# First projection of a two-layer decoder trunk: x in quarters, its weights in smaller transfers, casts between the evacuations

## The chip, the cores and the metric

One core of a Trainium2 chip. The metric is the device time of one execution in microseconds (us). The profile of the kernel before is one execution, recorded by the hardware profiler. Engines are called PE (matmul; PEld is its weight load), DVE (vector), ACT (scalar), POOL (gpsimd) and SP (which here only issues transfers).

## The reference

Two layers, each with RMSNorm, one input projection, three causal token mixers, an output projection, then RMSNorm and a gated MLP with a short convolution. All in float32, 256 tokens, width 1024. Only the first step of the first layer matters here:

```python
h = rmsnorm(x, norm1_g[i])                    # (1, 256, 1024)
(a_q, a_kc, ...) = jnp.split(h @ w_in[i], IN_OFFSETS, axis=-1)   # w_in[i]: 1024 x 2615
```

## The kernel before, in words

The 256 tokens are two tiles (t) of 128 partitions. `xr` holds x as tokens x 1024. For a projection PE needs x with its columns on the partitions, so `transposed` (L184) transposes 128-column blocks (four PE transposes for two blocks and two token tiles, into one PSUM bank of role "t", "s" or "o"), and evacuates each block: ACT writes `hi` (rounded to fp32r, times the norm's gain; L195), DVE writes the remainder `lo` (L196). Weights are split in the same way by `weight` (L148): a transfer on SP into a staging buffer `st` (five of them, NST), an ACT cast to `hi` (L158), a DVE subtraction for `lo` (L160). A staging buffer can be filled again when both have read it. `mm3` (L205) makes one product out of three: hi x hi, hi x lo, lo x hi.

The input projection runs in seven column blocks, by `project` (L273): block 0 has columns 0 to 384, the second (336 columns, `put_a1`) 384 to 720, the third (360 columns, `put_i`) 1103 to 1463, and so on. Each has four weight transfers (two 128-row pieces each) and 48 matmuls in eight steps k (two token tiles x three products). `fill` advances these generators a step at a time, between other work.

The norm's row scale isn't applied to x but at the evacuation of each block: `sumsq` (ACT, L179) and L258 (DVE) sum the squares of x, `rms` and `scales` make `rstd` and its multiples on POOL (L172 to L174, L265), and the `put_...` functions use them.

At the start, in layer 0: x comes in halves of columns, token tile by token tile; PE runs 16 idle matmuls on zeros (`idle`), transposes the gain columns (`columns`, L141), then the first half of x (L239, L242), then 8 more idle matmuls. Step 0 and 1 of block 0 follow (`fill(1)`, L569), then `second_half` transposes the second half of x behind the newest matmul, and the squares come behind its evacuations. The casts of the second block's weights are put behind the squares: `behind=squares` (L562), where `squares[0]` is the last of ACT and `squares[1]` the last of DVE.

The order on each engine is planned ahead by the framework's scheduler from the program's order and dependences, and is fixed when the kernel runs. `after(ins)` puts what the block issues behind `ins` on the engine of `ins`.

Of the kernel before, what the change touches and what calls it, by code (L numbers as in the profile page):

```python
# [12 lines left out]
F32 = mybir.dt.float32  # L13
FR = mybir.dt.float32r
# [6 lines left out]
D = 1024  # L21
# [5 lines left out]
AHEAD = 5  # L27
NST, NHL = 5, 8
# [42 lines left out]
def trunk(ctx, tc, x, norm1_g, w_in, cmp_pos, cmp_w1, cmp_w2, w_out, norm2_g, w_up, conv_w, conv_b, w_down,  # L71
          final_g, eye, consts_f, consts_b, out):
    nc = tc.nc
# [12 lines left out]
    turn = [0]  # L86
# [9 lines left out]
    xr = keep.tile([128, 2, D], F32, name="xr")  # L96
    ident = keep.tile([128, 128], F32, name="ident")
    rn = keep.tile([16, 128], F32, name="rows_n")
    nc.sync.dma_start(xr[:, 0, 0:512], x[0, 0:128, 0:512])
    nc.scalar.dma_start(xr[:, 1, 0:512], x[0, 128:256, 0:512])  # L100
    nc.sync.dma_start(ident, eye)
    nc.scalar.dma_start(rn, norm1_g.rearrange("l (f p) -> (l f) p", p=128))
    zero = keep.tile([128, 256], BF, name="zero")
    V.memset(zero, 0.0)
# [40 lines left out]
    def after(ins):  # L145
        return tc.issue_after(ins) if ins else nullcontext()
# [13 lines left out]
            V.tensor_sub(lv, sv, hv.bitcast(F32))  # L160
        return hv, lv

    def w_in_chunk(i, c0, n, then=(None,) * 4, behind=(None, None)):
        w = w_in[i].rearrange("(k p) c -> p k c", p=128)
        return [weight(w[:, 2 * h:2 * h + 2, c0:c0 + n], 2, n, then[h], behind) for h in range(4)]


    def rms(ss, name):
# [12 lines left out]
    def new_ssq():  # L181
        return keep.tile([128, 2, 2], F32, name="ssq", tag="ssq", bufs=2)

    def transposed(bank, src, gain, hi, lo, k0, nk, role="t"):  # L184

        b = bank(role)
        for j in range(nk):
            for t in range(2):
                PE.transpose(b[:, j * 256 + t * 128:j * 256 + (t + 1) * 128],
                             src[:, t, (k0 + j) * 128:(k0 + j + 1) * 128], ident)  # L190
        h, l = (z[k0 // 4][:, k0 % 4:k0 % 4 + nk, :] for z in (hi, lo))
        for j in range(nk):
            g = gain[:, k0 + j:k0 + j + 1]
            bj = b[:, j * 256:(j + 1) * 256]
            l0 = S.activation(h[:, j, :], bj, AF.Copy, scale=g)  # L195
            l1 = V.scalar_tensor_tensor(l[:, j, :], bj, g, h[:, j, :].bitcast(F32), op0=OP.mult, op1=OP.subtract)  # L196
        return l0, l1

    def act_half():
# [10 lines left out]
    for i in range(DEPTH):  # L210

        with ExitStack() as es:
# [5 lines left out]
            tmp = es.enter_context(tc.tile_pool(name="tmp", bufs=2, reuse_waits="tile"))  # L218

            w2 = pj.tile([128, 2, 64], F32, name="w2")  # L220
            first, squares = None, [None, None]
            if i == 0:

                def idle(n):
                    b = bank("d")
                    for j in range(n):
                        PE.matmul(b[:, :256], zero[:, 0:128], zero, start=j == 0, stop=j == n - 1)

                idle(16)
                columns(bank("t"), cola[:, 0:16], rn)  # L230


                def other_half():
                    for t in range(2):
                        nc.sync.dma_start(xr[:, t, 512:D], x[0, t * 128:(t + 1) * 128, 512:D])

                ssq = new_ssq()
                hhi, hlo = act_pair()
                two = transposed(bank, xr, gain1[i], hhi, hlo, 0, 2, role="t")  # L239
                first = w_in_chunk(0, 0, 384, (other_half, None, None, lambda: nc.sync.dma_start(cf, consts_f)),  # L240
                                   [z.ins for z in two])
                transposed(bank, xr, gain1[i], hhi, hlo, 2, 2, role="s")  # L242
                idle(8)
            rstd = None
            rs8, rs16, rsh = (pj.tile([128, 2], F32, name=f"rs{j}") for j in range(3))

            def second_half(behind):

                with after(behind):
                    for k0 in (4, 6):  # L250
                        last = transposed(bank, xr, gain1[0], hhi, hlo, k0, 2, role="so"[k0 // 2 - 2])
                for t in range(2):
                    with after(last[0].ins):
                        squares[0] = sumsq(ssq, t, 0).ins
                    junk = pj.tile([128, 512], BF, name="junkv", tag="selb")
                    xs = xr[:, t, 512:D]
                    with after(last[1].ins):
                        squares[1] = V.scalar_tensor_tensor(junk, xs, 1.0, xs, op0=OP.mult, op1=OP.mult,  # L258
                                                            accum_out=ssq[:, t, 1:2]).ins

            def scales():
                nonlocal rstd
# [7 lines left out]
                    if i == 0:  # L270
                        other_constants()

            def project(c0, n, done, wh=None, behind=(None, None), role="d"):  # L273
                wh = wh or w_in_chunk(i, c0, n, behind=behind)
                bs = [bank(role), bank(role)]
                for half in range(4):
                    for t in range(2):
                        for k in range(2):
                            kk = half * 2 + k
# [274 lines left out]
            def put_qk(r, dst):  # L554
                def put(t, b):
# [3 lines left out]
                    return lambda: evac(dst(t), turned([P_[:, a * 128:(a + 1) * 128] for a in range(3)]))  # L559
                return put  # L560

            dense += [project(0, 384, put_a0, first), project(384, 336, put_a1, behind=squares, role="s"),  # L562
                      project(1103, 360, put_i),
                      project(719, 384, put_b),
                      project(1463, 384, put_qk(lambda: rs8, lambda t: qT[:, t])),
                      project(1847, 384, put_qk(lambda: rstd, lambda t: kT[:, :, t, :])),
                      project(2231, 384, lambda t, b: a_put(vd[:, t, :], b[:, :384], rstd, t))]
            if i == 0:
                fill(1)  # L569
                second_half(newest[0].ins)  # L570
                scales()
                fill(17 + AHEAD)
            else:
                scales()
                fill(18 + AHEAD)
            V.tensor_scalar(gate, gate, 0.5, 0.5, op0=OP.mult, op1=OP.add)
            gt = gate.rearrange("p t (h c) -> p t h c", c=3)

# [453 lines left out]
```

## Time and profile before

| | us |
|---|---|
| median of 3 runs (lowest, highest) | 664.06 (661.97, 664.2) |
| the profiled execution | 662.68 |
| its span, first to last instruction | 660.9 |
| PE busy in the span | 641.7 |

Each row of the views below is one instruction or a run of equal ones. `bd<-hl,ahi` is the tile written and the tiles read; `[0.88 <-DVE qrT L521]` is idle time of the engine ahead of the instruction and what ended it. `SPq`, `POOLq` and a DMA_DIRECT2D on POOL are the issue of a transfer, not the transfer.

### The profile page before, as it was taken

What the parts mean: (1) busy time and instruction counts of PE and PEld (TensorE: products, weight loads), DVE (VectorE), ACT (ScalarE), POOL (GpSimd) and SP (SyncE); (2) the same over time, 40 slices, a digit from 0 to 9 for tenths busy, and PEclk for the clock granted to TensorE, in tenths of its full rate; (3) what the DMA queues carried; (4) which work ended last, traced back from release to release, by engine and by line L of the source; (5) the groups of instructions that cost most, each with busy time, mean ns of one, the idle gap of its engine ahead of it and who ended that gap; (6) DMA issues with size and microseconds to landing.
All of it is one profiled execution on the core that took longest, in us unless ns stands there. A gap on an engine that the chain in (4) does not pass through costs nothing.

```text
span 660.9 us, 11729 instructions
## 1 busy us (share of the span) xinstructions
PE 641.7 (97%) x4403; PEld 578.4 (88%) x4403; DVE 497.5 (75%) x1093; ACT 375.5 (57%) x683; POOL 50.3 (8%) x119
## 2 busy tenths in 40 slices
PE   8989999999999999999999999999999999999995
PEld 6978987779999999999898888877999999999994
DVE  5979998776766677777587799986697776666653
ACT  6666667775544444455475676785654455544523
POOL 0522210001000000000020242000000000000002
PEclk9999999999999999999999999999999999999998
DMA  8982423454665565565457525234465655566601
GB/s 268 279 265 72 126 83 113 134 184 158 192 188 185 179 188 184 182 182 160 128 167 228 149 71 176 81 110 155 127 218 189 184 182 182 187 191 190 191 1 63
DMA packets 76535, 107.34 MB, mean 162 GB/s; under 512 B 3717, under 2 KB 63414, under 8 KB 76480
## 3 DMA queue, kind: packets, MB, share of 16 engines
q1 hardware_dynamic: 75568, 104.77, 51.2%
q0 software_dynamic: 448, 1.05, 0.5%
q8 instruction: 34, 0.56, 0.3%
q10 hardware_dynamic: 464, 0.79, 0.3%
q14 instruction: 21, 0.17, 0.1%
HBM read 105.55 MB, written 1.05 MB: 161 GB/s over the span
## 4 chain that ended last, share of the span: by engine, by line
PE 81%; DVE 11%; DMA 2%; issue 2%; ACT 2%; POOL 1%; POOLq 0%; DVEq 0%; ACTq 0%
PE bu L921 13%; PE bu L920 13%; PE bu L919 13%; PE bn L206 6%; PE bn L207 6%; PE bn L208 6%; PE bd L206 5%; PE bd L208 5%; PE bd L207 5%; DVE hl L160 3%; PE bs L352 2%; DMA st<-in_w_in_dram 2%; PE bt L372 2%; PE bt L341 1%; DVE acc L484 1%
## 5 line engine op out<-in xcount | busy, mean ns | idle before, releaser
L160 DVE TENSOR_TENSOR hl<-st,hl 128x1024 fp32r<-128x1024 f32 (+3 forms) x208 | 230.7, 1120 | 97.3 <-ACT hl L158 96.8
L158 ACT CAST hl<-st 128x1024 fp32r<-128x1024 f32 (+3 forms) x208 | 198.0, 970 | 136.4 <-PE bu L921 68.1
L920 PE MATMUL bu<-alo,hl 128*128 128x256 f32 x704 | 199.7, 284 | 1.3 <-DVE alo L196 1.3
L921 PE MATMUL bu<-ahi,hl 128*128 128x256 f32 x704 | 199.0, 283 | 0.0
L919 PE MATMUL bu<-ahi,hl 128*128 128x256 f32 x704 | 197.9, 283 | 0.0
L920 PEld LDWEIGHTS bu<-alo,hl 128*128 128x128 f32 x704 | 135.1, 192 | 2.4 <-DVE alo L196 1.7
L919 PEld LDWEIGHTS bu<-ahi,hl 128*128 128x128 f32 x704 | 134.5, 192 | 1.3 <-ACT ahi L195 0.3
L921 PEld LDWEIGHTS bu<-ahi,hl 128*128 128x128 f32 x704 | 135.1, 192 | 0.0
L206 PE MATMUL bd<-hl,ahi 128*128 128x384 f32 (+2 forms) x256 | 92.9, 367 | 2.3 <-ACT hl L158 1.4
L207 PE MATMUL bd<-hl,ahi 128*128 128x384 f32 (+2 forms) x256 | 91.4, 357 | 0.4 <-DVE hl L160 0.4
L208 PE MATMUL bd<-hl,alo 128*128 128x384 f32 (+2 forms) x256 | 91.2, 356 | 0.0
L206 PE MATMUL bn<-hl,h_hi 128*128 128x512 f32 x176 | 68.9, 392 | 0.0
L207 PE MATMUL bn<-hl,h_hi 128*128 128x512 f32 x176 | 68.6, 391 | 0.0
L208 PE MATMUL bn<-hl,h_lo 128*128 128x512 f32 x176 | 68.4, 390 | 0.0
L206 PEld LDWEIGHTS bd<-hl,ahi 128*128 128x128 f32 x256 | 48.0, 188 | 11.0 <-ACT hl L158 3.0
L207 PEld LDWEIGHTS bd<-hl,ahi 128*128 128x128 f32 x256 | 48.2, 188 | 3.6 <-issue 0.8
L208 PEld LDWEIGHTS bd<-hl,alo 128*128 128x128 f32 x256 | 48.2, 188 | 3.1 <-issue 0.9
L208 PEld LDWEIGHTS bn<-hl,h_lo 128*128 128x128 f32 x176 | 33.0, 188 | 7.4 <-DVE h_lo L943 0.4
L206 PEld LDWEIGHTS bn<-hl,h_hi 128*128 128x128 f32 x176 | 33.1, 188 | 6.6 <-ACT h_hi L942 0.5
L207 PEld LDWEIGHTS bn<-hl,h_hi 128*128 128x128 f32 x176 | 33.1, 188 | 6.0
L931 DVE SCALAR_TENSOR_TENSOR c<-a,colc,c 128x255 f32<-128x255 f32 (+1 forms) x88 | 36.7, 477 | 0.7 <-ACT c L929 0.7
L934 ACT ACTIVATE th<-c 128x512 f32<-128x512 f32 x22 | 13.9, 632 | 35.1 <-DVE c L931 35.1
(242 smaller groups left out, 782.0 us busy)
## 6 DMA issues: line engine op xcount, KB each, us to landing
st<-in_w_up_dram SPq DMA_DIRECT2D x88, 512.0 KB, 3.6
st<-in_w_down_dram SPq DMA_DIRECT2D x44, 512.0 KB, 3.5
st<-in_w_in_dram SPq DMA_DIRECT2D x40, 384.0 KB, 3.8
st<-in_w_out_dram SPq DMA_DIRECT2D x12, 512.0 KB, 3.8
st<-in_w_in_dram SPq DMA_DIRECT2D x8, 360.0 KB, 3.5
st<-in_w_in_dram SPq DMA_DIRECT2D x8, 336.0 KB, 3.6
st<-in_w_out_dram SPq DMA_DIRECT2D x8, 256.0 KB, 3.0
xr<-in_x_dram SPq DMA_DIRECT2D x3, 256.0 KB, 5.9
```

Source lines behind the costliest of these rows:

```text
L158: S.copy(hv, sv)
L160: V.tensor_sub(lv, sv, hv.bitcast(F32))
L206: PE.matmul(b, ahi, whi, start=first, stop=False)
L207: PE.matmul(b, ahi, wlo, start=False, stop=False)
L208: return PE.matmul(b, alo, whi, start=False, stop=last)
L352: PE.matmul(b[:, o:o + nk], qa, ka, start=True, stop=True)
L372: PE.transpose(b[:, j * 128:(j + 1) * 128], P[:, j * 128:(j + 1) * 128], ident)
L919: PE.matmul(o, wa, hhi[k // 4][:, k % 4, :], start=k == 0, stop=False)
L920: PE.matmul(o, wa, hlo[k // 4][:, k % 4, :], start=False, stop=False)
L921: PE.matmul(o, wl, hhi[k // 4][:, k % 4, :], start=False, stop=k == 7)
L931: V.scalar_tensor_tensor(c[:, o + d:o + 256], a[:, o:o + 256 - d], cw[w], c[:, o + d:o + 256], op0=OP.mult, op1=OP.add)
L934: S.activation(th, c, AF.Tanh, scale=0.5)
```

## The change

Block 0 of layer 0 is no longer run by `project`'s loop but written out in `begin`, which is called while the list `dense` is made. x comes in four quarters of 256 columns, both token tiles in one transfer: quarter 0 on SP, quarters 1 to 3 on POOL's queue, with consts_f behind them. `ident` moves from SP to ACT's queue. The weights of quarter 0 come in two transfers of 192 KB, the others in three of 384 KB, all on SP. For each quarter, `transposed` gets a pair of weight pieces (`between`): after each evacuation on ACT the cast of one 384-column piece, after each one on DVE its lo. On PE the transposes of quarter q + 1 are put behind step 2q, ahead of step 2q + 1. The squares come behind the casts of the last quarter. The 8 idle matmuls go. `project` takes the finished banks (`bs`) for block 0 and then only calls `put_a0`; `fill` therefore has four steps less.

```diff
@@ -96,9 +96,13 @@
     xr = keep.tile([128, 2, D], F32, name="xr")
     ident = keep.tile([128, 128], F32, name="ident")
     rn = keep.tile([16, 128], F32, name="rows_n")
-    nc.sync.dma_start(xr[:, 0, 0:512], x[0, 0:128, 0:512])
-    nc.scalar.dma_start(xr[:, 1, 0:512], x[0, 128:256, 0:512])
-    nc.sync.dma_start(ident, eye)
+
+    def x_quarter(q, e):
+        c = slice(q * 256, (q + 1) * 256)
+        e.dma_start(xr[:, :, c], x[0, :, c].rearrange("(t p) c -> p t c", p=128))
+
+    x_quarter(0, nc.sync)
+    nc.scalar.dma_start(ident, eye)
     nc.scalar.dma_start(rn, norm1_g.rearrange("l (f p) -> (l f) p", p=128))
     zero = keep.tile([128, 256], BF, name="zero")
     V.memset(zero, 0.0)
@@ -160,9 +164,9 @@
             V.tensor_sub(lv, sv, hv.bitcast(F32))
         return hv, lv
 
-    def w_in_chunk(i, c0, n, then=(None,) * 4, behind=(None, None)):
+    def w_in_chunk(i, c0, n, behind=(None, None)):
         w = w_in[i].rearrange("(k p) c -> p k c", p=128)
-        return [weight(w[:, 2 * h:2 * h + 2, c0:c0 + n], 2, n, then[h], behind) for h in range(4)]
+        return [weight(w[:, 2 * h:2 * h + 2, c0:c0 + n], 2, n, None, behind) for h in range(4)]
 
 
     def rms(ss, name):
@@ -181,7 +185,8 @@
     def new_ssq():
         return keep.tile([128, 2, 2], F32, name="ssq", tag="ssq", bufs=2)
 
-    def transposed(bank, src, gain, hi, lo, k0, nk, role="t"):
+    def transposed(bank, src, gain, hi, lo, k0, nk, role="t", between=None):
+
 
         b = bank(role)
         for j in range(nk):
@@ -194,6 +199,12 @@
             bj = b[:, j * 256:(j + 1) * 256]
             l0 = S.activation(h[:, j, :], bj, AF.Copy, scale=g)
             l1 = V.scalar_tensor_tensor(l[:, j, :], bj, g, h[:, j, :].bitcast(F32), op0=OP.mult, op1=OP.subtract)
+            if between:
+                sv, hv, lv = (z[:, j] for z in between)
+                with after(l0.ins):
+                    l0 = S.copy(hv, sv)
+                with after(l1.ins):
+                    l1 = V.tensor_sub(lv, sv, hv.bitcast(F32))
         return l0, l1
 
     def act_half():
@@ -218,7 +229,7 @@
             tmp = es.enter_context(tc.tile_pool(name="tmp", bufs=2, reuse_waits="tile"))
 
             w2 = pj.tile([128, 2, 64], F32, name="w2")
-            first, squares = None, [None, None]
+            squares = [None, None]
             if i == 0:
 
                 def idle(n):
@@ -229,26 +240,42 @@
                 idle(16)
                 columns(bank("t"), cola[:, 0:16], rn)
 
-
-                def other_half():
-                    for t in range(2):
-                        nc.sync.dma_start(xr[:, t, 512:D], x[0, t * 128:(t + 1) * 128, 512:D])
-
                 ssq = new_ssq()
                 hhi, hlo = act_pair()
-                two = transposed(bank, xr, gain1[i], hhi, hlo, 0, 2, role="t")
-                first = w_in_chunk(0, 0, 384, (other_half, None, None, lambda: nc.sync.dma_start(cf, consts_f)),
-                                   [z.ins for z in two])
-                transposed(bank, xr, gain1[i], hhi, hlo, 2, 2, role="s")
-                idle(8)
+            first = None
             rstd = None
             rs8, rs16, rsh = (pj.tile([128, 2], F32, name=f"rs{j}") for j in range(3))
 
-            def second_half(behind):
-
-                with after(behind):
-                    for k0 in (4, 6):
-                        last = transposed(bank, xr, gain1[0], hhi, hlo, k0, 2, role="so"[k0 // 2 - 2])
+            def begin():
+
+                w = w_in[0].rearrange("(k p) c -> p k c", p=128)
+                wh = []
+                for h in range(4):
+                    st = wst.tile([128, 1024], F32, name="st", tag="st", bufs=NST)
+                    hl = wst.tile([128, 2048], FR, name="hl", tag="hl", bufs=NHL)
+                    sv, hv, lv = (z.rearrange("p (k n) -> p k n", k=2) for z in (st[:, :768], hl[:, :768], hl[:, 1024:1792]))
+                    for k in range(2) if h == 0 else [slice(0, 2)]:
+                        nc.sync.dma_start(sv[:, k], w[:, k, 0:384] if h == 0 else w[:, 2 * h:2 * h + 2, 0:384])
+                    if h:
+                        x_quarter(h, nc.gpsimd)
+                    wh.append((sv, hv, lv))
+                nc.gpsimd.dma_start(cf, consts_f)
+                bs = [bank("d"), bank("d")]
+                last = [None, None]
+
+                def turn(q):
+                    return transposed(bank, xr, gain1[0], hhi, hlo, 2 * q, 2, role="tsst"[q], between=wh[q])
+
+                turn(0)
+                for kk in range(8):
+                    q, k = kk // 2, kk % 2
+                    for t in range(2):
+                        c = slice(t * 128, (t + 1) * 128)
+                        mm = mm3(bs[t][:, :384], hhi[kk // 4][:, kk % 4, c], hlo[kk // 4][:, kk % 4, c],
+                                 wh[q][1][:, k], wh[q][2][:, k], kk == 0, kk == 7)
+                    if k == 0 and q < 3:
+                        with after(mm.ins):
+                            last = turn(q + 1)
                 for t in range(2):
                     with after(last[0].ins):
                         squares[0] = sumsq(ssq, t, 0).ins
@@ -257,6 +284,7 @@
                     with after(last[1].ins):
                         squares[1] = V.scalar_tensor_tensor(junk, xs, 1.0, xs, op0=OP.mult, op1=OP.mult,
                                                             accum_out=ssq[:, t, 1:2]).ins
+                return bs
 
             def scales():
                 nonlocal rstd
@@ -270,10 +298,13 @@
                     if i == 0:
                         other_constants()
 
-            def project(c0, n, done, wh=None, behind=(None, None), role="d"):
-                wh = wh or w_in_chunk(i, c0, n, behind=behind)
-                bs = [bank(role), bank(role)]
-                for half in range(4):
+            def project(c0, n, done, bs=None, behind=(None, None), role="d"):
+                if bs is None:
+                    wh = w_in_chunk(i, c0, n, behind=behind)
+                    bs, halves = [bank(role), bank(role)], range(4)
+                else:
+                    halves = ()
+                for half in halves:
                     for t in range(2):
                         for k in range(2):
                             kk = half * 2 + k
@@ -559,20 +590,14 @@
                     return lambda: evac(dst(t), turned([P_[:, a * 128:(a + 1) * 128] for a in range(3)]))
                 return put
 
-            dense += [project(0, 384, put_a0, first), project(384, 336, put_a1, behind=squares, role="s"),
+            dense += [project(0, 384, put_a0, bs=begin() if i == 0 else None), project(384, 336, put_a1, behind=squares, role="s"),
                       project(1103, 360, put_i),
                       project(719, 384, put_b),
                       project(1463, 384, put_qk(lambda: rs8, lambda t: qT[:, t])),
                       project(1847, 384, put_qk(lambda: rstd, lambda t: kT[:, :, t, :])),
                       project(2231, 384, lambda t, b: a_put(vd[:, t, :], b[:, :384], rstd, t))]
-            if i == 0:
-                fill(1)
-                second_half(newest[0].ins)
-                scales()
-                fill(17 + AHEAD)
-            else:
-                scales()
-                fill(18 + AHEAD)
+            scales()
+            fill((14 if i == 0 else 18) + AHEAD)
             V.tensor_scalar(gate, gate, 0.5, 0.5, op0=OP.mult, op1=OP.add)
             gt = gate.rearrange("p t (h c) -> p t h c", c=3)
```

## Rows read from the trace of the kernel before

**Rows 1.** The page: the span, and the busy time of each engine with its share and its instructions.

```profile
span 660.9 us, 11729 instructions
PE 641.7 (97%) x4403; PEld 578.4 (88%) x4403; DVE 497.5 (75%) x1093; ACT 375.5 (57%) x683; POOL 50.3 (8%) x119
```

**Rows 2.** Stretches of 20 us: length, busy time of PE, PEld, DVE, ACT and POOL (instructions), granted clock of PE as a share of full speed, busy share of the 16 DMA engines, GB/s.

```profile
0.00:20.00 20.00, 17.02 (x101) 14.98 (x102) 12.37 (x26) 13.09 (x24) 4.31 (x16) 1.00 0.78 253
20.00:40.00 20.00, 16.99 (x120) 15.69 (x122) 16.86 (x49) 12.15 (x25) 6.07 (x12) 1.00 1.01 312
40.00:60.00 20.00, 18.91 (x169) 17.28 (x159) 16.79 (x43) 13.64 (x25) 5.92 (x11) 1.00 0.56 165
```

**Rows 3.** The same columns for single microseconds.

```profile
5.00:6.00 1.00, 1.00 (x10) 0.98 (x11) 0.17 (x1) 0.41 (x1) 0.00 (x0) 1.00 0.64 209
...
7.00:8.00 1.00, 0.00 (x0) 0.00 (x0) 0.50 (x2) 0.70 (x2) 0.00 (x0) 1.00 1.06 398
...
12.00:13.00 1.00, 1.00 (x7) 1.00 (x7) 1.00 (x3) 1.00 (x3) 0.62 (x2) 1.00 0.51 128
...
17.00:18.00 1.00, 1.00 (x8) 1.00 (x7) 1.00 (x3) 1.00 (x3) 0.91 (x2) 1.00 0.12 41
...
19.00:20.00 1.00, 1.00 (x9) 1.00 (x8) 1.00 (x2) 0.34 (x1) 0.83 (x3) 1.00 1.01 354
```

**Rows 4.** The chain of waits from 0 to 50 us: start, us, what. "issue" is time in which nothing that the profile shows was waited for.

```profile
15.11 0.62 DVE junkv L258 x2
...
17.90 0.86 DVE hl L160
...
18.78 5.00 DMA st<-in_w_in_dram
...
37.58 2.13 issue
```

**Rows 5.** The timeline of PE: start, us, line, operation, count.

```profile
1.04 3.56 PE L227 MATMUL bd<-zero 128*128 128x256 bf16 x16 [1.04 <-DVE kbd L635]
...
4.89 0.66 PE L189 MATMUL bt<-ident,xr 128*128 128x128 f32 x4
...
5.82 1.04 PE L227 MATMUL bd<-zero 128*128 128x256 bf16 x8
...
8.27 0.62 PE L206 MATMUL bd<-hl,ahi 128*128 128x384 f32 x2 [1.41 <-ACT hl L158]
...
14.09 0.33 PE L206 MATMUL bd<-hl,ahi 128*128 128x384 f32 x1
...
14.26 0.33 PE L207 MATMUL bd<-hl,ahi 128*128 128x384 f32 x1
...
18.25 0.31 PE L206 MATMUL bs<-hl,ahi 128*128 128x336 f32 x1
...
25.69 0.55 PE L341 MATMUL bt<-ident,PA 128*128 128x128 f32 x3 [0.88 <-DVE qrT L521]
...
39.71 1.95 PE L607 MATMUL bo<-w,raw 128*32 128x128 f32 x64 [2.13 <-issue]
```

**Rows 6.** The timeline of ACT and DVE, 5 to 20 us, the same columns.

```profile
5.00 0.17 DVE L142 COPY cola<-bt 128x16 f32<-128x16 f32 x1 [3.95 <-PE bt L141]
...
5.59 0.47 ACT L195 ACTIVATE ahi<-bt,cola 128x256 fp32r<-128x256 f32 x1 [2.43 <-PE bt L189]
...
7.38 0.83 ACT L158 CAST hl<-st 128x768 fp32r<-128x768 f32 x1 [0.30 <-DMA st<-in_w_in_dram]
...
9.83 0.83 ACT L158 CAST hl<-st 128x768 fp32r<-128x768 f32 x1 [1.24 <-DMA st<-in_w_in_dram]
...
12.58 0.48 DVE L196 SCALAR_TENSOR_TENSOR alo<-bs,cola,ahi 128x256 fp32r<-128x256 f32 x1
...
12.98 0.48 DVE L196 SCALAR_TENSOR_TENSOR alo<-bo,cola,ahi 128x256 fp32r<-128x256 f32 x1
...
13.49 0.48 ACT L195 ACTIVATE ahi<-bo,cola 128x256 fp32r<-128x256 f32 x1
...
13.86 0.62 ACT L179 ACTIVATE junk<-xr 128x512 bf16<-128x512 f32 x1
...
15.24 3.48 ACT L158 CAST hl<-st 128x672 fp32r<-128x672 f32 x5
...
16.36 3.99 DVE L160 TENSOR_TENSOR hl<-st,hl 128x672 fp32r<-128x672 f32 x5
```

**Rows 7.** The timeline of SP's and POOL's queues: issue of transfers (start, us that the issue took; a wait lies in it where the buffer or an earlier transfer isn't ready), and POOL's last memset of the start.

```profile
0.89 0.20 POOL L457 MEMSET acc<- 128x128 f32 x1
...
4.17 1.36 SPq L154 DMA_DIRECT2D st<-in_w_in_dram  x2
...
21.46 0.77 POOL L269 DMA_DIRECT2D w<-in_cmp_w_dram  x1
```

**Rows 8.** Transfers by line: tile and source, queue, count, KB each, median us from issue to landing.

```profile
fg<-in_final_g_dram POOLq DMA_DIRECT2D x1, 512.0 KB, 4.0
...
cb<-in_consts_b_dram POOLq DMA_DIRECT2D x1, 256.0 KB, 8.0
```

## Prediction

> **What bounds the kernel now.** Read the page's busy times first: TensorE (PE) is busy 641.7 of 660.9 us [rows 1]. So there are 19 us of idle PE to win in the whole kernel, and the change touches only the first 18 us of it. Next read the stretches of 20 us [rows 2]: in 0 to 20 PE is busy 17.0 us, but between 20 and 40 it is again only 17.0, with the transfers at 1.01 of the DMA engines' time. From 40 us on PE is nearly full. So two different things limit the start: until 18 us PE waits for its first operands, and from 19 to 38 us the kernel is bound by transfers. The single microseconds [rows 3] show where DMA time is lost ahead of that: the share is 0.64 at 5 us, 0.51 at 12 us and 0.12 at 17 us, and 1.01 from 19 us on. The chain of waits [rows 4] says why 17 us is empty. The squares of x on DVE at 15.11 us are followed by the rest (lo) of the second block's weights, 17.90 to 18.77, which frees a staging buffer, and only then, at 18.78, is the next weight transfer issued. It lands 5.00 us later, and the path stays with weights and DVE up to the PE wait of 2.13 us at 37.58. In the timeline of PE the first projection starts at 8.27 and hands over to the second block at 18.25 without a pause [rows 5].
>
> So the number to forecast is not when PE starts, but when the second block's casts free the staging buffers: in the kernel before, 18.78 us.
>
> **The change part by part.**
>
> **Loads.** The first operands become smaller: one x quarter of 256 KB and 192 KB of weights, in place of 512 KB and 384 KB. Quarters 1 to 3 and consts_f go past SP to POOL's queue. SP had to hold two weight transfers until x had landed (issue at 4.17) [rows 7], which is the dip at 5 us [rows 3]; with four SP transfers fewer ahead of them they go out sooner, and about 0.6 us of lost DMA time is regained. No sum needs it, because the last weights already landed ahead of their use. The total bytes are the same.
>
> How late x quarter 1 lands (X1) is not shown before. The nearest rows are POOL's own transfers: 0.77 us of issue for a 256-row one [rows 7], and landing after 4.0 us (512 KB, quiet) to 8.0 us (256 KB, DMA full) [rows 8]. POOL is free at 1.1 us [rows 7], so X1 lies between 5.1 and 9.1; I take 6.5, nearer to the quiet end, because the DMA engines are filled by fewer bytes at that time. The Trainium skill ("DMA: Bandwidth & Descriptors", section "Anatomy of one DMA — SWDGE (gpsimd) path") fits a POOL transfer as 2.0 us plus bytes over 436 GB/s; by that estimate 2.6 us after a 0.8 us issue, X1 would be 4.5 and never late. The rows, at twice that and more, leave a late X1 possible.
>
> The weights of quarter 1 (H1) have at least 1.12 MB ahead of or in them (x quarter, ident, half blocks, themselves) and, if POOL takes an equal share, 1.9 MB. The kernel before landed its first 384 KB of weights (0.99 MB in) at 7.38 and its second (1.9 MB in) at 9.83 [rows 6], so H1 is 7.4 to 9.8; I take 8.5. The same skill page (section "Issuing engines are not separate DMA queues") says that transfers of all queues run on the same 16 engines and that several queues save issue time only; by it three queues bring nothing here but the 0.6 us.
>
> **Start.** The gain columns still come at 5.00 + 0.17 us, from a transfer that keeps its place on ACT's queue, so the first evacuation starts between 5.19 and 5.59 [rows 6]; I take 5.59. The cast of 384 columns isn't shown: on ACT it lies between the step of a 256-column evacuation, 13.86 - 13.49 = 0.37, and that of a 672-column cast, 3.48 / 5 = 0.70; by width 0.48. On DVE between 12.98 - 12.58 = 0.40 and 3.99 / 5 = 0.80; by width 0.50 [rows 6]. So hi of the first block is ready at 5.59 + 0.37 + 0.48 = 6.5 and lo at 7.0, against 8.27 and 9.26 before. PE starts 1.8 us earlier. The 8 idle matmuls taken away (5.82 to 6.86 [rows 5]) lay in a wait and cost nothing.
>
> **First block.** A step k is 6 matmuls at 14.26 - 14.09 = 0.17 us, 1.04; it ends step 0 at 7.9. After that PE runs: four transposes (0.44 of PE time, 0.60 to the last end), step 1, step 2, transposes, step 3, step 4. But step 2 needs evacuation, cast and lo of the transposes just made: 0.65 + 0.37 + 0.48 + 0.07 + 0.55 = 2.1 us after their start, where PE has work for 0.44 + 1.04 + 0.17 = 1.65. So each turn takes 2.1 + 0.87 = 3.0 us, or 2.8 where PE takes the second hi product ahead (it did so at 8.27 [rows 5]), against 2.5 of work. Step 4 ends at 7.9 + 2 x 2.8 = 13.5. I call this time T4; it is 12.5 with the earliest start and no stall. With X1 at 9.1 it is 9.1 + 5.8 = 14.9; with H1 at 9.8 it is 14.6.
>
> **What is queued behind.** The last quarter's transposes are put behind step 4, the squares behind the last quarter's casts, and the second block's casts behind the squares. Before, the second half of x was transposed after step 0, at 10.2 us, so this chain began early. Now it begins at T4. On ACT: transposes and semaphore 0.65; two evacuations and two casts 2 x (0.37 + 0.48) = 1.7; squares 15.24 - 13.86 = 1.4; first cast of the second block 0.7. On DVE then three lo's at 0.8, the third of which frees the buffer of the last weights of the third block: 2.4. Together 6.9 us: issue at T4 + 6.9 = 20.4 against 18.78 [rows 4]. Behind these casts stand PE (second block) and SP (all later weights); the row scales on POOL follow the squares too, and so slip by the same amount. Break-even is T4 = 11.9; even the earliest case, 12.5, misses it. PE itself ends the first block at T4 + 3.5 = 17.0 instead of 18.25, and then waits for the second block's lo until T4 + 4.5 + 0.8 = 18.8: what is won in the block is idle again.
>
> **Sum.** 20.4 - 18.8 = +1.6 us at the entry of the stretch that is bound by transfers. That passes through: DMA is at 1.01 there, PE waits 2.13 us at 39.71 for work behind weights [rows 4, 5], and later PE has at most 1.1 us of idle in 20 to take it up [rows 2]. The eight casts in place of four (+0.8 us on ACT, +0.5 on DVE) are inside this. The profiled execution took 662.68 us (span 660.9 and 1.8 around it), the median shown is 664.06. So the sum is 664.3 by the profile and 665.7 by the median; I give 665.0.
>
> **The rivals.**
> 1. *The earlier PE start counts, the later weights are hidden.* For it: the wait at 25.69 is only 0.88 us [rows 5], and the DMA engines had holes at 12 and 17 us [rows 3] which the new order may fill differently. PE could then keep 18.25 - 17.0 = 1.2 us: 662.68 - 1.2 = 661.5 by the profile, 662.8 by the median. Against it: the squares must come before the second block's casts in either kernel. Chance 0.18.
> 2. *Slower: x quarter 1 comes late from POOL's queue.* Place: the transposes of the first turn, ahead of step 1 in PE's order, so every later matmul waits. Price: each us of X1 beyond 7.9 is one us of T4. The end of the POOL rows, 9.1, gives +3.0 us; at 10.5, where the queue is starved by SP's 1.5 MB, +4.4: 667.1 by the profile, 668.5 by the median. It decides from X1 = 9.5 on (+3.3). Chance 0.13.
> 3. *The clock.* Without the 8 idle matmuls PE pauses about 1 us before step 0. The first 16 ran 3.56 / 16 = 0.22 us each (1.2 GHz for 256 columns), the later 8 at 0.13 (near 2.4) [rows 5]. If it fell back, 30 matmuls up to T4 would cost 0.15 more each: +4.4, 668. Against it: after the pauses at 8.27 and 39.71 (1.4 and 2.1 us) nothing ran slower, and the granted clock is 1.00 in all these rows [rows 2, 3]. Chance 0.03.
> 4. *A different static order later on.* The order on each engine is planned as a whole, so the waits at 25.69 and 39.71 may vanish or grow: -3 to +3 us about the forecast. Chance 0.12, half each way.
>
> **How the numbers follow.** Forecast 0.54, rivals 0.18, 0.13, 0.03, 0.12. 0.5% (3.3 us) is about what a measurement of this kernel can tell from no change. The forecast's own bounds, T4 of 12.5 to 14.9, are +0.6 to +3.0: all within. Within 0.5%: 0.54 + 0.18 + 0.04 of the fourth = 0.76. Slower: rivals 2 and 3 and a part of 4, 0.18. Faster than that needs the first rival and both later waits gone (1.2 + 0.9 + 2.1): 0.06. The range runs from rival 1 by the profile, 661.5, to rival 2 by the median, 668.5.
>
> **What would show it.** Right: first projection matmul near 6.5; the last transposes of x near 13.5; squares on ACT near 15.9; a PE pause of about 1 us between first and second block; third block's last weights issued near 20.4; the whole timeline later by 1 to 2 us at the first cmp_w1 matmuls (39.71 before). Wrong: squares before 14 us, or no pause and the cmp_w1 matmuls at or before 39.7 (rival 1); transposes of quarter 1 waiting for a POOL transfer beyond 8 us (rival 2); a matmul step of 0.3 us in the first block (rival 3).

## The result and the profile after

The changed kernel takes 668.52 us (median of 6 runs, 667.84 to 670.17) against 663.84 (661.97 to 664.2) for the kernel before: by the means of the runs a ratio of 1.0079, 95% interval 1.006 to 1.0098. It is slower by 0.8%, clear of the noise; the forecast, 665.0 with a range up to 668.5, said no change. The profiled execution took 669.91 us. Its page has the span, the busy times and the granted clock in 40 slices:

```profile
span 667.9 us, 11725 instructions
PE 646.8 (97%) x4395; PEld 579.0 (87%) x4395; DVE 498.8 (75%) x1097; ACT 375.2 (56%) x687; POOL 51.2 (8%) x123
PEclk9979999999999999999999999999999999999998
```

Of the 7.0 us that the span grew, PE's busy time took 5.1 (641.7 before [rows 1]) and its idle time 1.9. A PE that is busy longer with fewer matmuls (the 8 idle ones are gone) runs slower somewhere, and the third slice, 33 to 50 us, has a clock of 0.7.

Next, where the two timelines part for good. The first MLP matmul of layer 0 in the timeline of PE, before and then changed:

```profile
143.56 0.52 PE L919 MATMUL bu<-ahi,hl 128*128 128x256 f32 x3
```

```profile
150.41 0.51 PE L944 MATMUL bu<-ahi,hl 128*128 128x256 f32 x3
```

The lag is 6.8 us there and 7.0 at the end. So all of it arises ahead of the MLP. The timeline of PE in the changed kernel at the places that the forecast named:

```profile
6.36 0.62 PE L217 MATMUL bd<-hl,ahi 128*128 128x384 f32 x2 [0.96 <-ACT hl L205]
6.95 0.44 PE L218 MATMUL bd<-hl,ahi 128*128 128x384 f32 x1
...
7.40 0.34 PE L218 MATMUL bd<-hl,ahi 128*128 128x384 f32 x1
7.58 0.34 PE L219 MATMUL bd<-hl,alo 128*128 128x384 f32 x1
...
13.79 0.60 PE L194 MATMUL bt<-ident,xr 128*128 128x128 f32 x4
...
18.40 0.58 PE L217 MATMUL bs<-hl,ahi 128*128 128x336 f32 x2 [0.44 <-ACT hl L162]
19.29 0.42 PE L218 MATMUL bs<-hl,ahi 128*128 128x336 f32 x1 [0.32 <-DVE hl L164]
...
22.65 0.55 PE L372 MATMUL bt<-ident,PA 128*128 128x128 f32 x3 [1.56 <-DVE PA L342]
...
42.53 0.66 PE L217 MATMUL bd<-hl,ahi 128*128 128x384 f32 x1 [2.67 <-DVE PI L342]
```

Up to 19.29 all is as forecast. The next rows are ACT's timeline, to be laid beside [rows 6], where the squares are followed by five casts in a row:

```profile
16.23 0.63 ACT L183 ACTIVATE junk<-xr 128x512 bf16<-128x512 f32 x1
...
16.98 0.63 ACT L183 ACTIVATE junk<-xr 128x512 bf16<-128x512 f32 x1
...
17.61 1.39 ACT L162 CAST hl<-st 128x672 fp32r<-128x672 f32 x2
21.21 1.48 ACT L339 ACTIVATE QR<-bd,rs 128x640 f32<-128x640 f32 x2 [2.21 <-POOL rs L293]
22.58 1.40 ACT L162 CAST hl<-st 128x672 fp32r<-128x672 f32 x2
```

Here only two casts of the second block follow the squares. Then comes the evacuation QR of block 0, which waits 2.21 us for the row scales from POOL, and the third and fourth cast stand behind it. The third cast frees the buffer for the last weights of the third block. Its transfer, the eighth that SP issues on this line (3.70, 7.96, 10.91, 13.98, 16.95, 19.27, 20.04, then this one), goes out here:

```profile
25.28 0.37 SPq L158 DMA_DIRECT2D st<-in_w_in_dram  x1
```

That is 25.28 against 18.78 before [rows 4] and 20.4 in the forecast. The view by stretches (busy us of each engine with instruction counts; last columns: granted clock, DMA share, GB/s) shows the DMA engines nearly empty in 14 to 15 and 17 to 18 us, a share of 0.82 in 20 to 40 where it was 1.01 [rows 2], and the clock at half from 42 us on:

```profile
20.00:40.00 20.00, 18.11 (x117) 16.52 (x115) 15.88 (x47) 12.40 (x25) 6.14 (x13) 1.00 0.82 253
40.00:60.00 20.00, 17.37 (x136) 15.10 (x136) 14.31 (x30) 11.72 (x23) 5.43 (x13) 0.83 0.79 245
14.00:15.00 1.00, 1.00 (x9) 1.00 (x8) 0.07 (x1) 0.57 (x2) 0.00 (x0) 1.00 0.03 8
17.00:18.00 1.00, 0.96 (x6) 0.64 (x4) 0.96 (x3) 1.00 (x3) 0.00 (x0) 1.00 0.11 7
40.00:42.00 2.00, 0.00 (x0) 0.00 (x0) 1.96 (x4) 1.75 (x5) 0.07 (x1) 1.00 1.06 319
42.00:44.00 2.00, 1.47 (x14) 1.03 (x18) 1.84 (x5) 1.37 (x4) 1.92 (x6) 0.54 1.04 301
44.00:46.00 2.00, 2.00 (x30) 1.55 (x23) 1.77 (x3) 0.07 (x1) 1.82 (x3) 0.50 1.05 370
46.00:48.00 2.00, 2.00 (x7) 2.00 (x7) 0.00 (x0) 1.59 (x3) 0.00 (x0) 0.50 1.05 349
48.00:50.00 2.00, 2.00 (x36) 1.36 (x36) 0.00 (x0) 0.83 (x1) 0.00 (x0) 0.75 0.39 146
```

A clock of 0.50 is 1.2 GHz, 1.00 is 2.4. The clock time lost is 2 x (0.46 + 0.50 + 0.50 + 0.25) = 3.4 us in this execution, a little of it while PE still waits. It follows the PE pause of 2.67 us ahead of 42.53.

### The profile page after: what moved, and what is told of

It reads as the page before. It is cut to its first block, busy times and chain, and to the rows that moved or that the text cites. A ratio compares the mean times of both kernels' runs of the same rounds, so it can differ in the third digit from the quotient of the medians.

```text
span 667.9 us, 11725 instructions
## 1 busy us (share of the span) xinstructions
PE 646.8 (97%) x4395; PEld 579.0 (87%) x4395; DVE 498.8 (75%) x1097; ACT 375.2 (56%) x687; POOL 51.2 (8%) x123
## 4 chain that ended last, share of the span: by engine, by line
PE 80%; DVE 12%; ACT 3%; issue 2%; POOL 1%; DMA 1%; POOLq 0%; ACTq 0%; DVEq 0%; SPq 0%
PE bu L945 13%; PE bu L946 13%; PE bu L944 13%; PE bn L217 6%; PE bn L218 6%; PE bn L219 6%; PE bd L217 5%; PE bd L219 4%; PE bd L218 4%; DVE hl L164 3%; PE bt L403 2%; PE bs L383 1%; PE bo L755 1%; DVE P L777 1%; ACT hl L162 1%
## 5 line engine op out<-in xcount | busy, mean ns | idle before, releaser
L164 DVE TENSOR_TENSOR hl<-st,hl 128x1024 fp32r<-128x1024 f32 (+3 forms) x204 | 227.5, 1126 | 93.4 <-ACT hl L162 92.9
L162 ACT CAST hl<-st 128x1024 fp32r<-128x1024 f32 (+3 forms) x204 | 194.6, 972 | 136.4 <-PE bu L946 68.2
```

What stands on the lines that cost most here:

```text
L162: S.copy(hv, sv)
```

## The experiments

The theory to test was that the loss comes from the new order of work: the row scales' evacuation stands ahead of two casts on ACT, the weights behind them go out late, PE pauses at 40 us and then runs at half clock. The rivals: the loads on three queues; the late squares by themselves; and the place of the first cmp_w1 transfers in SP's order. Times are medians; ratios are of means, to runs of the kernel before on the same chip (its medians there: 663.3 for e1, e2, e3 and e5; 662.9 for e4, e6, e7 and e8; 663.3 for the rest).

**e1_loads_alone.** The kernel before with the new loads only: quarters, smaller transfers, three queues.

```diff
+    x_quarter(0, nc.sync)
+    nc.scalar.dma_start(ident, eye)
...
-                first = w_in_chunk(0, 0, 384, (other_half, None, None, lambda: nc.sync.dma_start(cf, consts_f)),
+                first = w_in_chunk(0, 0, 384, (None, lambda: x_quarter(1, nc.gpsimd), lambda: x_quarter(2, nc.gpsimd), last_loads),
```

> The kernel before with only the new loads (x in quarters, ident on ACT, first weights in two pieces, quarters 1 to 3 and consts_f from POOL's queue); the order of the work is the old one. Theory A (the loss is in the new order of the work: transposes, squares and casts come late, the loads are harmless): 661.5 to 664.5 us, squares on ACT before 14.5 us. Theory B (the loads from POOL's queue and their contention cost the time): 666 us or more, with transposes of x waiting beyond 8 us.

Measured: 663.93 us, ratio 1.001 (1.0002 to 1.0019); first MLP matmul at 144.46. From the timelines of ACT and PE:

```profile
16.16 0.62 ACT L184 ACTIVATE junk<-xr 128x512 bf16<-128x512 f32 x1
...
17.53 2.71 ACT L163 CAST hl<-st 128x672 fp32r<-128x672 f32 x4
21.60 0.79 ACT L313 ACTIVATE QR<-bd,rs 128x640 f32<-128x640 f32 x1 [1.36 <-PE bd L213]
```

```profile
7.93 1.12 PE L194 MATMUL bs<-ident,xr 128*128 128x128 f32 x4 [1.92 <-DMA xr<-in_x_dram]
```

PE waits 1.92 us for a quarter of x from POOL, and the squares, at 16.16, are as late as in the changed kernel (16.23) and not before 14.5 as expected, yet the kernel loses only 0.7 us. All four casts stand ahead of the scales' evacuation here. So the loads do not make the loss, and in the old order of work late squares do not either.

**e2_order_alone.** The changed kernel with the loads of the kernel before (halves of x, whole transfers, SP and ACT).

```diff
-                    for k in range(2) if h == 0 else [slice(0, 2)]:
-                        nc.sync.dma_start(sv[:, k], ...)
-                    if h:
-                        x_quarter(h, nc.gpsimd)
+                    nc.sync.dma_start(sv, w[:, 2 * h:2 * h + 2, 0:384])
```

> The changed kernel with the loads of the kernel before; only the new order of the work is left. Theory A (order): 666.5 to 670 us, squares on ACT at 16 us or later. Theory B (loads): 662 to 665 us.

Measured: 667.07 us, 1.0061 (1.0048 to 1.0074). The squares come at 17.44. Three casts precede the evacuation here (18.83), which waits 2.02 us until 22.89. The order without the new loads is 3.8 us over the kernel before, the loads without the order 0.7. But not all of the 3.8 us need be the order: in this execution the first block runs at half clock, as it does not in the changed kernel.

```profile
8.00:10.00 2.00, 2.00 (x9) 1.90 (x8) 0.19 (x2) 0.61 (x2) 0.00 (x0) 0.50 1.07 391
```

**e3_casts_first.** The changed kernel, with `put_a0` behind all four casts of the second block on ACT and DVE.

```diff
+                with after(halves == () and newcast[0]), after(halves == () and newcast[1]):
+                    fs = [done(t, bs[t]) for t in range(2)]
...
+            ahead = w_in_chunk(0, 384, 336, behind=squares) if i == 0 else None
```

> The changed kernel, but the evacuations of block 0 by put_a0 are put behind all four casts of the second block on ACT and on DVE; in the changed kernel ACT waits 2.2 us for the row scales with two of these casts behind it. Theory A1 (this wait in ACT's fixed order is a main part of the loss): 664.5 to 666.5 us, no PE pause near 21 us. Theory A2 (only the late start of the squares counts, the 6.9 us chain behind it being as it was): 667.5 to 669 us.

Measured: 665.19 us (11 runs), 1.0033 (1.002 to 1.0046). ACT's and SP's timelines:

```profile
17.46 2.70 ACT L162 CAST hl<-st 128x672 fp32r<-128x672 f32 x4
21.57 1.48 ACT L342 ACTIVATE QR<-bd,rs 128x640 f32<-128x640 f32 x2 [1.40 <-POOL rs L295]
```

```profile
20.66 1.40 SPq L158 DMA_DIRECT2D st<-in_w_in_dram  x1
```

The third block's last weights go out at 20.66, near where the forecast had them (20.4), and the time is near the forecast time (665.0). In the profiled execution, the fastest of the eleven (663.89), the pause at 40 us is 1.53 instead of 2.67, with no half clock behind it. By the medians 3.3 us are won back. The dependence moved more than the casts: PE's planned order differs from the changed kernel's from 20 us on.

**e5_pe_kept_busy.** The changed kernel with 20 idle matmuls on zeros in the pause at 40 us.

```diff
+                        b = bank("o")
+                        for j in range(20):
+                            PE.matmul(b[:, :256], zero[:, 0:128], zero, start=j == 0, stop=j == 19)
```

> The changed kernel with 20 idle matmuls of 256 columns behind the transposes of cmp_pos, where PE pauses from 39.9 to 42.5 us and the granted clock is then 0.50 until about 49 us. Theory C (the pause lets the clock fall, and that is a part of the loss): granted clock 1.00 from 40 to 50 us, the profiled span 664 to 666 in place of 667.9, the median 1 to 3 us below the changed kernel's. Theory D (the low clock has nothing to do with the pause): the clock is again near 0.5 there and the time is 668 to 670.

Measured: 666.84 us, 1.0048 (1.0035 to 1.0061), 1.7 us less than the changed kernel. The clock is 1.00 from 40 to 50 us. The last weights still go out at 25.86. PE's order is another one from 42 us on (the cmp_w1 matmuls come first), so the 1.7 us are not a clean price of the clock; e12 gives a cleaner one.

**e4_turns_early.** The changed kernel; the last quarter's transposes behind step 2 instead of step 4, to bring squares and scales forward.

```diff
-                    if k == 0 and q < 3:
+                    if k == 0 and q < 2:
...
-                            last = turn(q + 1)
+                            for z in range(q + 1, 2 + 2 * q):
+                                last = turn(z)
```

> The changed kernel with the transposes of the last quarter put behind step 2 instead of step 4; ACT has three casts ahead of the evacuation of block 0 and one behind it. Theory A2 (late squares): T4 falls by some 3 us, squares on ACT near 13.5, time 664.5 to 666. Theory A1 (ACT's order): one cast instead of two behind the wait, so a part of the 3.3 us that the casts put first gave back: 666 to 667.5, and the squares are limited by the landing of the last weights, not by PE.

Measured: 664.4 us (11 runs), 1.003 (1.0017 to 1.0043). Squares at 14.96, three casts ahead of the evacuation, last weights at 19.61.

**e6_both.** e3 and e4 together.

> The changed kernel with all casts of the second block ahead of the evacuation of block 0, and the last quarter's transposes behind step 2. If the remaining 1.9 us over the kernel before is the late start of the squares: 662.5 to 664. If it is something later (the place of the second cmp_w1 transfer, the order of PE): 664.5 to 665.7, as with the casts put first alone.

Measured: 664.71 us (12 runs), 1.0028 (1.0015 to 1.0042). In the profiled execution the squares come at 16.17, not earlier than in the changed kernel (why is said at e12), so it does not add the two gains; last weights at 20.81.

**e7_w1_together.** e3 with both cmp_w1 transfers side by side on SP, as before.

```diff
+                w1s = []
+                for c in range(2):
+                    w1s.append(wst.tile([128, 16, 128], F32, name="w1", tag="hl", bufs=NHL))
+                    nc.sync.dma_start(w1s[c], cmp_w1[i, c].rearrange("(j p) h -> p j h", p=128))
```

> The changed kernel with all casts of the second block first, and the two cmp_w1 transfers issued one behind the other, as in the kernel before (in the changed kernel four to five weight transfers stand between them); layer 1 gets the same. If the place of the second transfer is the remaining 1.9 us: 662.5 to 664. If not: 664.5 to 666, or more where the weights of the fourth block land later for it.

Measured: 666.15 us, 1.0049 (1.0036 to 1.0062). No gain over e3: the split of these transfers (22.77 and 35.36 in e3) is not what remains.

**e8_before_scales_first.** The kernel before, with its third and fourth cast of the second block put behind the scales' evacuation, on ACT and DVE: the changed kernel's order there, without the change.

```diff
-            dense += [project(0, 384, put_a0, first), project(384, 336, put_a1, behind=squares, role="s"),
+            dense += [project(0, 384, put_a0, first), project(384, 336, put_a1, behind=[squares, squares, puts, puts] if i == 0 else squares, role="s"),
```

> The kernel before in all but one thing: the third and fourth cast of the second block are put behind the evacuations of block 0, on ACT and DVE, which is where the changed kernel has them. ACT then waits for the row scales with two casts behind it. Theory A1 (this place in ACT's order is a main cause of the loss): 665.5 to 668 us, ratio 1.003 to 1.007, although nothing else of the change is in it. Theory A2 (the late start of the squares is the cause): the squares start as early as before, so 662.5 to 664.5, ratio below 1.002.

Measured: 660.58 us, 0.9964 (0.9952 to 0.9977): faster than both kernels, and below what either theory expected. ACT's timeline:

```profile
13.47 0.64 ACT L180 ACTIVATE junk<-xr 128x512 bf16<-128x512 f32 x1
...
14.86 1.40 ACT L158 CAST hl<-st 128x672 fp32r<-128x672 f32 x2
18.68 1.48 ACT L309 ACTIVATE QR<-bd,rs 128x640 f32<-128x640 f32 x2 [2.42 <-POOL rs L266]
20.05 1.41 ACT L158 CAST hl<-st 128x672 fp32r<-128x672 f32 x2
```

The same evacuation in the kernel before:

```profile
19.66 1.48 ACT L308 ACTIVATE QR<-bd,rs 128x640 f32<-128x640 f32 x2 [0.94 <-POOL rs L265]
```

ACT waits even longer (2.42 us) with two casts behind it, the third block's last weights go out at 22.74 instead of 18.78, and the kernel gains 2.3 us. The evacuation itself comes at 18.68, against 19.66 in the profile of the kernel before, and PE has none of the pause at 25.69 [rows 5]; that these two are what the gain consists of was not tested apart. So the place in ACT's order is not a loss by itself; the theory in that simple form fell.

**e9_changed_again.** The changed kernel, unaltered, beside the next three.

> The changed kernel unaltered, for a second profile. In the first one the granted clock was 0.50 from 42 to 49 us behind a PE pause of 2.67 us. Theory C (the low clock is a main part of the loss in every run): it is there again and the span is 667 to 668. Theory E (it comes in some executions only; what stays is 4 us without it): no row below 0.9 between 5 and 140 us and the span is 665 to 666.

Measured: 668.62 us, 1.0081 (1.0069 to 1.0093). In this execution the pause at 40 us is 2.05 us, and the clock behind it is lower for half as long as in the first:

```profile
40.00:50.00 10.00, 8.14 (x88) 6.91 (x89) 6.81 (x13) 6.03 (x11) 3.81 (x8) 0.83 0.84 272
```

**e10_before_no_idle8.** The kernel before without its 8 idle matmuls (one line, `idle(8)`, taken out).

> The kernel before without the 8 idle matmuls that the change takes away; nothing else. As predicted (they lie in a wait): ratio 0.998 to 1.002. Rival 3 (they keep the clock up): a granted clock below 1.00 in the first block and 1 to 4 us more.

Measured: 663.46 us (12 runs), 1.0004 (0.9995 to 1.0013). The first 20 us by stretches:

```profile
0.00:10.00 10.00, 6.89 (x30) 4.77 (x31) 3.54 (x11) 4.97 (x9) 0.56 (x9) 0.90 0.76 271
10.00:20.00 10.00, 10.00 (x59) 9.90 (x59) 9.07 (x16) 8.03 (x16) 3.77 (x7) 0.93 0.73 232
```

The granted clock is lower at the start here, by 10 x (0.10 + 0.07) = 1.7 us in all, and the time does not change: what is lost there does not reach the end of this kernel.

**e11_changed_idle8.** The changed kernel with 8 idle matmuls after the first transposes.

```diff
+                b = bank("o")
+                for j in range(8):
+                    PE.matmul(b[:, :256], zero[:, 0:128], zero, start=j == 0, stop=j == 7)
```

> The changed kernel with 8 idle matmuls again behind the first transposes. If the clock at the start is a part of the loss: 1 to 3 us below the changed kernel. If not: the same as the changed kernel within 1 us, or some tenths more, since the idle matmuls may now stand ahead of step 0.

Measured: 667.87 us, 1.0065 (1.0052 to 1.0078), an interval that overlaps the changed kernel's (1.0069 to 1.0093 in e9). The pause at 40 us (2.62) and the half clock behind it (0.66 over 40 to 50 us) stay.

**e12_early_scales_first.** e4, with the third and fourth cast put behind the evacuation again.

```diff
+            puts = [None, None]
-            dense += [..., project(384, 336, put_a1, behind=squares, role="s"),
+            dense += [..., project(384, 336, put_a1, behind=[squares, squares, puts, puts] if i == 0 else squares, role="s"),
```

> The changed kernel with the last quarter's transposes behind step 2 (squares about 1.3 us earlier) and the evacuation of block 0 behind two casts on ACT, as in the changed kernel and in the kernel before with the scales first. Theory F (the two act together: late scales cost nearly nothing behind four casts, and several us behind two): time between 660.6 and 668.5 by how late the squares are, 663 to 666. Theory G (what is left over the kernel before comes from begin's order as a whole): 664 to 665.5 whatever the squares do.

Measured: 666.37 us, 1.005 (1.0038 to 1.0062). In the profiled execution the squares came no earlier after all (16.17), so it became another run than meant: the changed kernel's order on ACT at the same time, with a shorter pause at 40 us and the full clock behind it. Timelines of ACT and PE, the stretch from 40 to 50 us, and in the last fence PE in e9:

```profile
17.57 1.40 ACT L162 CAST hl<-st 128x672 fp32r<-128x672 f32 x2
21.23 1.48 ACT L341 ACTIVATE QR<-bd,rs 128x640 f32<-128x640 f32 x2 [2.26 <-POOL rs L295]
```

```profile
7.98 0.53 PE L220 MATMUL bd<-hl,alo 128*128 128x384 f32 x1
8.30 0.53 PE L219 MATMUL bd<-hl,ahi 128*128 128x384 f32 x1
...
41.74 0.41 PE L218 MATMUL bd<-hl,ahi 128*128 128x384 f32 x1 [1.88 <-DVE PI L344]
...
146.75 0.52 PE L948 MATMUL bu<-ahi,hl 128*128 128x256 f32 x3
```

```profile
40.00:50.00 10.00, 8.26 (x100) 7.36 (x101) 7.76 (x15) 6.92 (x13) 3.84 (x8) 1.00 0.92 284
```

```profile
41.86 0.41 PE L217 MATMUL bd<-hl,ahi 128*128 128x384 f32 x1 [2.05 <-DVE PI L342]
...
148.41 0.52 PE L944 MATMUL bu<-ahi,hl 128*128 128x256 f32 x3
```

Two things follow. First, the matmuls of the first block start 0.32 us apart here (7.98 to 8.30), the pace of e2 at half clock, against 0.18 in the changed kernel (7.40 to 7.58). The first blocks of e6 and e1 have the same slow pace. That is why the squares of e12 and e6 are no earlier in these executions, while e4's (14.96), at the full pace, are. The clock column reads 1.00 in such rows at the start, in e12 and e6 as in [rows 2], where 16 idle matmuls ran at 0.22 us each [rows 5]; at the start the pace of the matmuls is the surer sign.

Second, this run prices the clock at 40 us. From 19 us on e12 runs the same instructions in the same order on PE, ACT and DVE as the two profiles of the changed kernel, and until 39 us within 0.1 us of them. The changed kernel lies 0.8 us behind e12 at the end of the pause (42.53 against 41.74) and 3.7 at the first MLP matmul (150.41 against 146.75): 2.9 us more, behind a clock of 0.50. In e9 it is 0.1 and 1.7: 1.5 us more, with half as much low clock.

## Why the prediction failed, point by point

**Start and first block: right.** First matmul 6.36 (forecast 6.5), first with lo 6.95 (7.0), T4 13.79 (13.5), squares 16.23 (15.9), second block's lo 19.29 (18.8), PE pause there 0.44 + 0.32 = 0.8 us (1).

**Loads: right in effect.** POOL's quarters of x landed 6.5 us after their issue (median of the three), the transposes of quarter 1, at 7.75, wait for nothing (bound for X1: 7.9), and the loads alone cost 0.7 us (e1). The Trainium skill ("DMA: Bandwidth & Descriptors", section "Issuing engines are not separate DMA queues") says that transfers issued from different engines run on the same 16 DMA engines and that issuing them from several saves issue time only. The runs agree as far as they go: in e1 the loads from three queues gain nothing. The same page's fit for a POOL transfer (section "Anatomy of one DMA — SWDGE (gpsimd) path"), 2.6 us by the forecast's estimate, is far below the measured 6.5; the measurement decides. Rival 2 did not come about: that the measured 668.52 lies at its price, 668.5, is chance.

**Two steps failed.** The first is the one in "What is queued behind" that ends "Together 6.9 us: issue at T4 + 6.9 = 20.4". It took the third cast, whose lo frees the buffer, to follow the squares directly, as in the kernel before. In the changed kernel the planner put block 0's evacuation between the second and the third cast, that evacuation waited for the row scales, and the issue came at 25.28, 4.9 us later. With the four casts first (e3) it is 20.66. I had seen that the row scales slip with the squares, but not that a cast could stand behind what waits for them.

The second is the clock, which the sum puts at nothing (rival 3, at the start only, had 0.03). Behind the pause at 40 us it fell to 0.50, which cost 2.9 us in the first profile and 1.5 us in e9 (both against e12). Of the 3.5 us between the forecast and the measured median, 2.2 us separate the changed kernel from e12, which has the same order from 19 us on and whose profiled execution, the median one, has no half clock there; 1.2 us separate e12 from e3, which has the casts first. The rest is 0.2.

That e3's 665.19 us is so near the forecast is in part luck, since the next step did not hold as a rate.

**"That passes through"** failed as a general rule. The medians beside the time at which the third block's last weights go out (QR is block 0's evacuation on ACT, the casts are the second block's):

| order of block 0 | kernel | casts ahead of QR | issue, us | median, us |
|---|---|---|---|---|
| old | before | 4 | 18.78 | 663.3 |
| old | e10 | 4 | 18.77 | 663.46 |
| old | e1 | 4 | 21.06 | 663.93 |
| old | e8 | 2 | 22.74 | 660.58 |
| `begin` | e4 | 3 | 19.61 | 664.4 |
| `begin` | e3 | 4 | 20.66 | 665.19 |
| `begin` | e6 | 4 | 20.81 | 664.71 |
| `begin` | e7 | 4 | 21.25 | 666.15 |
| `begin` | e2 (old loads) | 3 | 22.02 | 667.07 |
| `begin` | e12 | 2 | 25.29 | 666.37 |
| `begin` | e5 | 2 | 25.86 | 666.84 |
| `begin` | e11 | 2 | 25.33 | 667.87 |
| `begin` | changed, e9 | 2 | 25.28, 25.21 | 668.52, 668.62 |

With the old order 2.3 us of lateness cost 0.7 (e1), and 4.0 us came with a gain (e8). With `begin`, those that issue up to 21.25 take 664.4 to 666.2, the later ones 666.4 to 668.6. The forecast's own figure, 1.6 for 1.6, has no support as a rate. One of its premises was not read from a row: the wait of 2.13 us at 39.71 was put down to weights, but [rows 4, 5] name no releaser for it ("issue").

**Rival 4, a different static order, is a part of what happened.** It had 0.12, at 3 us either way about the forecast. Putting the casts first is worth 3.3 us (e3), but 2.2 of these are the difference to e12, the clock above all; the 1.2 us left for the order lie within the price.

**Rival 3, the clock, was right in kind and wrong in place.** It looked at the 8 idle matmuls at the start, where a lower clock costs nothing (e10) and where putting them back gains nothing clear of the noise (e11), and it took the full clock behind two pauses of the kernel before as a reason that there would be none. Its sign, a matmul step of 0.3 us in the first block, is not in the changed kernel (0.18) but in e2, e6 and e12 (0.32), and not in e4, whose start is that of e6 and e12.

**What stays open.** Every kernel with `begin` is slower than the kernel before, by 0.28% (e6) to 0.81%. The 1.5 to 2 us that e3, e4 and e6 keep are not the place of cmp_w1 (e7) and not T4 alone (e4 has squares at 14.96 and the ratio of e3); the loads alone cost 0.7 (e1). A part can be placed: from 60 to 140 us PE is busy 0.9 us less in e3 than in the kernel before (first the kernel before, then e3).

```profile
60.00:140.00 80.00, 79.05 (x490) 63.40 (x489) 71.67 (x260) 55.36 (x145) 7.35 (x20) 1.00 0.36 111
```

```profile
60.00:140.00 80.00, 78.13 (x483) 62.25 (x482) 71.54 (x265) 55.36 (x145) 7.19 (x16) 1.00 0.35 112
```

e3 has PE pauses of 0.2 to 0.5 us between 88 and 123 us; which element of the planned order makes them was not tried, nor was `begin` with the later order of the kernel before. Why the pause at 40 us differs between executions of one order (2.67, 2.05, 1.88), and what decides whether the clock falls behind it, stays open too.

**The best version** is e8: 660.58 us, 0.36% under the kernel before, with none of the change's code in it.

## What to carry to other kernels

When part of a statically planned program is rewritten, the old trace does not show the new order: for each instruction that waits on a long chain (here squares, POOL, scales), price the sum both with the buffer-freeing work ahead of it and behind it, and give the worse one a real chance. If the order matters, fix it by a dependence and time both; the better side can differ between two versions of one kernel (e3 gains from casts first, e8 from scales first). Two runs that have the same order and part at one place price what happens there, as e9 and e12 do for the clock; a version whose order moved elsewhere too does not. A shift at the entry of a transfer-bound stretch is not the shift at its end.

## What the runs showed of the hardware

Half clock after a pause is not a matter of the pause's length alone. It followed pauses of 2.67, 2.05 and 2.62 us at 40 us in three profiles of the changed kernel's order (first profile, e9, e11), with 3.4, 1.7 and 3.4 us of clock time lost, but not one of 2.13 us in the kernel before [rows 5], one of 2.61 us at 39.84 in e10, or one of 1.88 us in e12. In e8, the fastest kernel, a pause of only 1.14 us was followed by a clock of 0.50:

```profile
54.62 1.22 PE L475 MATMUL bs<-ik,iq 128*128 128x256 f32 x4 [1.14 <-DVE iq L471]
```

```profile
55.00:57.00 2.00, 2.00 (x8) 1.93 (x8) 1.65 (x6) 1.49 (x4) 1.54 (x4) 0.50 0.00 0
```

The pauses of 0.96 us at the start were followed by half clock in e2 (0.50 in 8 to 10 us) and not in the changed kernel (1.00, and the matmuls at full pace).
